# Products of gate and up formed at once, transposed two to three units later, and no accumulating DMA in the first pair block

## Chip, cores and metric

The kernel runs on one core of a Trainium2 chip. The time is device microseconds of one execution, and the measure is the median of several runs. Before the change it is 1096.01 us (three runs, 1095.95 to 1096.87).

## What is computed

The reference is one layer of a streaming encoder on 256 tokens of width 2048: a block of differential attention and convolution, and behind it a gated feed-forward network. The change touches the feed-forward network alone:

```python
hn = rms_norm(h, norm2_g[l])
a = jnp.einsum('bsd,df->bsf', hn, w_gate[l])        # 2048 -> 5632
bu = jnp.einsum('bsd,df->bsf', hn, w_up[l])         # 2048 -> 5632
h = h + jnp.einsum('bsf,fd->bsd', jax.nn.silu(a) * bu, w_down[l])
```

All inputs are float32.

## The kernel before, in words

Every float32 operand is split in two, a rounded high part and a low part that is the difference, and a product of two such operands is three matmuls: high by high, low by high, high by low. The weights are split on the way: the SP queue loads a tile `raw`, ScalarE (ACT) rounds it to `whi` (L305), and VectorE (DVE) subtracts to get `wlo` (L314). For a few tiles, those in `BY_DMA` (L74), `wlo` is made otherwise: ACT writes the rounded negative of `raw` (L308), and a DMA issued from the POOL queue adds `raw` to it in place (L309); the subtraction on DVE then falls away.

The 5632 hidden columns are 11 blocks j of 512, in three groups of 4, 4 and 3 (`FGROUPS`). The blocks of a group are computed one after the other, then the group's share of the down projection is added (`block(w_down, ...)`, in chunks of two rows of 128, four column blocks of 512). Block 0 is computed plainly, gate and then up. Blocks 1 to 10 ("pairs" here, since gate and up are done together) use a fast scheme in `fast_block`: half of the 16 row tiles of the weights go through seven products of sums of tiles instead of eight (units of kind s, four in a pair, 21 matmuls each), the other half plainly (units g for gate and u for up, four each, 12 matmuls each). So a pair has twelve units, and the order is a string: `ORDER` "sggsggsuusuu" for pairs 2 to 10, `FIRST` "gugusgsgsusu" for pair 1. Below, a unit is named by kind and place in its pair, s0, g1, g2, s3 and so on. An s unit costs DVE three subtractions that form the sums of weights (L875 to L877) and two that form low parts (L883, L884), and ACT two roundings (L878, L879); L884 waits for L879, and L879 for L877.

A pair gathers in eight PSUM banks: Q1, Q6, Q7 and Q5 in the pool `acc` (four banks), Q2, Q4, Q3 and QX in the pool `aux` (four banks). A bank is handed out in the order in which banks were given back. When the pair's last s unit is done, `products_done` combines the banks (L962 to L972), and after its last unit `block_done` adds Q3 and QX (two DVE instructions, L980) and multiplies by the activated gate (two more, L983). `transposed` then turns the 128x512 product around on PE in two steps t, each four transposes into one bank `ps_a` (L794), a rounding copy `ahi` on ACT (L796) and a subtraction `alo` on DVE (L798). Here the two steps are called T0 and T1. For pairs their bank is from `aux`, for block 0 from `acc`.

The order on every engine is written out by the program. `run_chunks` goes over the units: ahead of the matmuls of unit t it emits the low parts of unit t+2 and the load, sums and rounding of unit t+3 (for plain chunks, t+2). Work such as `block_done` is a generator, taken one `yield` further at each `resume()`: in a g or u unit or a plain chunk in the middle and at the end, in an s unit behind products 2, 4, 6 and 7, and once more at the end of a pair. `lag(n)` lets n such points go by. If a matmul needs an operand whose `alo` has not been emitted yet, `operand` calls `resume()` until it has.

Of the kernel before, what the change touches and what calls it, by code (L numbers as in the profile page):

```python
# [73 lines left out]
BY_DMA = TWOS[-1:]  # L74

ORDER = "sggsggsuusuu"

FIRST = "gugusgsgsusu"

Q1, Q6, Q7, Q5, Q2, Q4, Q3, QX = range(8)  # L80

PRODUCTS = ((Q1, 0, 5), (Q6, 5, 1), (Q7, 6, 2), (Q5, 4, 3), (Q2, 1, 6), (Q4, 3, 0), (Q3, 2, 4))

HI_AHEAD, LO_AHEAD = 3, 2


def rope_constants():
# [10 lines left out]
def tile_block(  # L98
# [34 lines left out]
    rows = pre.tile([NR, P], F32, tag="rows", name="rows", bufs=1)  # L133
# [79 lines left out]
    def lhs_two(pfx, k):  # L213
        return tuple(lhs.tile([P, 2, S], F32R, tag=f"l{x}", name=f"{pfx}{x}{k}") for x in ("hi", "lo"))
# [20 lines left out]
    def lag(n):  # L235
        for _ in range(n):
            yield
# [538 lines left out]
    def up_done(j, ps):  # L776
        fp = ffn["pool"]
        yield
        aa = []
        for m in range(NM):  # L780
            a = fp.tile([P, N], F32, tag=f"sum{2 + m}", name="a")
            dve.scalar_tensor_tensor(a, ps[m], rstd2[m], sil[m], ALU.mult, ALU.mult)
            aa.append(a)
        yield
        yield from transposed(j, aa)

    def transposed(j, aa):
        for t in range(N // P // 2):
            pool_, tag = (aux_ps, "aux") if j else (acc_ps, "acc")
            pt = pool_.tile([P, 2, S], F32, tag=tag, name="ps_a")  # L790
            for i in range(2):
                for m in range(NM):
                    c = (2 * t + i) * P
                    pe.transpose(pt[:, i, m * P : (m + 1) * P], aa[m][:, c : c + P], ident)  # L794
            hi, lo = lhs_two("a", j * (N // P) + 2 * t)
            act.copy(hi, pt)  # L796
            yield
            dve.tensor_tensor(lo, pt, hi.bitcast(F32), ALU.subtract)  # L798
            for i in range(2):
                actT[j * (N // P) + 2 * t + i] = (hi[:, i, :], lo[:, i, :])  # L800
            yield

# [124 lines left out]
    def fast_block(j, order, after_down):  # L929

        units, sums = [], {}
        left = dict(s=list(range(NS)), g=list(TWOS), u=list(TWOS))
        for kind in order:
            what = left[kind].pop(0)
            c = dict(kind=kind, sums=sums, done=None, first={}, last={})
            if kind == "s":
                c.update(k=what, col=j * N, load=load_pair, round=round_pair, split=split_pair,
                         multiply=multiply_pair, uses=[q for q, _, _ in PRODUCTS], products=PRODUCTS)
            else:
                c.update(ks=what, w=w_gate if kind == "g" else w_up, nk=2, width=N, cols=[(j * N, N)],  # L940
                         rows=slice(what[0], what[1] + 1, what[1] - what[0]), by_dma=what in BY_DMA,
                         load=load_chunk, round=round_chunk, split=split_chunk, multiply=multiply_two,
                         uses=(Q3, QX) if kind == "u" else (Q2, Q4))
            units.append(c)
        assert not any(left.values())
        if after_down:

            units[0]["products"] = PRODUCTS[4:] + PRODUCTS[:4]
        for q in range(8):
            users = [c for c in units if q in c["uses"]]  # L950
            users[0]["first"][q] = users[-1]["last"][q] = True
        [c for c in units if c["kind"] == "s"][-1]["done"] = products_done
        units[-1].update(done=lambda sums: block_done(j, sums), prompt=True)
        chunks.extend(units)
# [20 lines left out]
    def block_done(j, q):  # L975
        while "g" not in halfway:
            yield
        g, u = halfway.pop("g"), halfway.pop("u")
        for m, i in enumerate((Q3, QX)):
            dve.tensor_tensor(u[m], q[i], u[m], ALU.add)  # L980
        yield
        for m in range(NM):
            dve.tensor_tensor(u[m], u[m], g[m], ALU.mult)  # L983
        yield from lag(2)
        yield from transposed(j, u)

    def down_done(g, n, ps):
# [35 lines left out]
    for g, nb in enumerate(FGROUPS):  # L1023
        for j in range(j0, j0 + nb):
            if j:
                fast_block(j, FIRST if j == 1 else ORDER, j == j0)
                continue

            block(w_gate, j * N, range(KD), fh, silu_done)
            block(w_up, j * N, range(KD), fh, lambda ps, j=j: up_done(j, ps))  # L1030
        for n in range(D // N):
            at = len(chunks)
            block(w_down, n * N, range(j0 * 4, (j0 + nb) * 4), fa, lambda ps, g=g, n=n: down_done(g, n, ps))
            for i, c in enumerate(chunks[at:]):
                c["prompt"] = True
                c["spare_raw"] = i % 3 == 2
        j0 += nb
# [32 lines left out]
```

## Time and profile before

| | |
|---|---|
| median of three runs | 1096.01 us |
| the profiled execution, its own time | 1098.23 us |
| its span, first to last instruction | 1096.4 us |
| mean granted TensorE clock | 0.993 of full |
| PE busy | 1063.8 us |
| VectorE (DVE) busy | 844.6 us |
| ScalarE (ACT) busy | 590.3 us |
| HBM read | 200.04 MB |

The feed-forward part runs from about 353 us to the end: block 0 up to 399 us, pairs 1 to 3 up to 540 us, a down stage, pairs 4 to 7 from 630 to 803 us, a down stage, pairs 8 to 10 from 891 to 1022 us, the last down stage. A row of the timeline gives start, duration, engine, line, operation, output and input, shape, and in brackets the idle time of the engine ahead of it with what ended it. Durations of matmuls overlap: in a full stream they start 0.23 us apart. DVE instructions overlap a little as well, so the distance of two starts is the better measure there.

### The profile page before, as it was taken

Reading aid. Unit: us, or ns where it says so; the run is one execution under the profiler, and the core shown is the slowest. Engines: PE = TensorE matmul, PEld = TensorE weight load, DVE = VectorE, ACT = ScalarE, POOL = GpSimd, SP = SyncE. Lnnn points to the kernel's source line nnn. Section 1 sums busy time; section 2 is a strip of 40 time slices with the busy share of each in tenths; the row PEclk is TensorE's granted clock in tenths of the full one; section 3 lists DMA queues with packets and bytes.
Section 4 is the critical chain, followed back from the end, with each engine's and each line's share of the span. In section 5 each row is a group of like instructions: output and inputs, shape, how many; then the busy total and the mean of one; then the engine's idle time right before and its main releaser. Section 6 shows DMA issues by size and latency. Waiting matters only on the chain.

```text
span 1096.4 us, 13237 instructions
## 1 busy us (share of the span) xinstructions
PE 1063.8 (97%) x4834; PEld 873.6 (80%) x4834; DVE 844.6 (77%) x1023; ACT 590.3 (54%) x767; POOL 64.7 (6%) x103
## 2 busy tenths in 40 slices
PE   8999999999999998899999999999999999999998
PEld 7888888877888886687788887877878888778786
DVE  4799989898755779988654699988855589988553
ACT  6544567756764655555443456556533355565332
POOL 0030021201000000000000000000000000000000
PEclk9999999999999999899999999999999999999999
DMA  8756655544345567576455776866646568666561
GB/s 242 251 178 205 192 174 173 154 154 154 135 173 194 171 211 248 181 236 186 147 206 181 247 242 202 248 208 194 186 160 211 201 221 264 213 194 185 170 232 66
DMA packets 121229, 213.50 MB, mean 195 GB/s; under 512 B 7252, under 2 KB 29198, under 8 KB 121164
## 3 DMA queue, kind: packets, MB, share of 16 engines
q1 hardware_dynamic: 117744, 200.56, 54.8%
q0 software_dynamic: 3360, 12.06, 5.9%
q8 instruction: 38, 0.62, 0.2%
q14 instruction: 27, 0.22, 0.1%
q10 hardware_dynamic: 60, 0.03, 0.0%
HBM read 200.04 MB, written 2.10 MB: 184 GB/s over the span
## 4 chain that ended last, share of the span: by engine, by line
PE 85%; DVE 8%; DMA 3%; issue 3%; ACT 1%; POOL 1%; SPq 0%; DVEq 0%; POOLq 0%; ACTq 0%
PE acc L350 16%; PE acc L345 16%; PE acc L344 16%; PE q L917 6%; PE q L918 6%; PE q L923 6%; PE q L900 5%; PE q L902 5%; PE q L901 5%; DVE wlo L314 2%; DVE sum L983 1%; DMA raw<-in_w_in_dram 1%; PE ps_a L794 1%; DVE sum L980 1%; DMA raw<-in_w_gate_dram 1%
## 5 line engine op out<-in xcount | busy, mean ns | idle before, releaser
L305 ACT CAST whi<-raw 128x1024 fp32r<-128x1024 f32 (+1 forms) x297 | 309.9, 1048 | 266.1 <-PE acc L345 171.1
L314 DVE TENSOR_TENSOR wlo<-raw,whi 128x1024 fp32r<-128x1024 f32 (+1 forms) x277 | 335.8, 1218 | 148.5 <-ACT whi L305 148.5
L344 PE MATMUL acc<-whi,ahi 128*128 128x512 f32 x384 | 150.6, 392 | 0.0
L345 PE MATMUL acc<-whi,alo 128*128 128x512 f32 x384 | 150.4, 392 | 0.0
L879 ACT CAST wh<-wt 128x2048 fp32r<-128x2048 f32 x40 | 76.5, 1912 | 104.6 <-DVE wt L877 104.6
L344 PE MATMUL acc<-whi,xhi 128*128 128x512 f32 (+1 forms) x352 | 130.1, 376 | 2.8 <-ACT xhi L219 2.5
L345 PE MATMUL acc<-whi,xlo 128*128 128x512 f32 (+1 forms) x352 | 128.7, 372 | 0.5 <-DVE xlo L220 0.4
L917 PE MATMUL q<-whi,chi 128*128 128x512 f32 x320 | 126.6, 396 | 0.0
L918 PE MATMUL q<-whi,clo 128*128 128x512 f32 x320 | 126.2, 394 | 0.0
L902 PE MATMUL q<-wl,fhi 128*128 128x512 f32 x280 | 110.1, 393 | 2.0 <-DVE wl L884 2.0
L900 PE MATMUL q<-wh,fhi 128*128 128x512 f32 x280 | 110.7, 396 | 0.0
L901 PE MATMUL q<-wh,flo 128*128 128x512 f32 x280 | 109.3, 390 | 0.0
L481 DVE SCALAR_TENSOR_TENSOR y<-upad,cw,y 128x256 f32<-128x256 f32 x240 | 103.3, 480 | 2.8 <-ACT y L474 2.3
L350 PE MATMUL acc<-wlo,ahi 128*128 128x512 f32 x384 | 103.6, 391 | 0.0
L884 DVE TENSOR_TENSOR wl<-wt,wh 128x2048 fp32r<-128x2048 f32 x40 | 91.6, 2290 | 8.4 <-ACT wh L879 8.1
L923 PE MATMUL q<-wlo,chi 128*128 128x512 f32 x320 | 87.3, 395 | 2.4 <-DMA wlo<-raw 2.4
L350 PE MATMUL acc<-wlo,xhi 128*128 128x512 f32 (+1 forms) x352 | 88.5, 377 | 1.2 <-DVE wlo L314 1.2
L345 PEld LDWEIGHTS acc<-whi,alo 128*128 128x128 f32 x384 | 72.7, 189 | 15.2
L344 PEld LDWEIGHTS acc<-whi,ahi 128*128 128x128 f32 x384 | 72.5, 189 | 15.2
L350 PEld LDWEIGHTS acc<-wlo,ahi 128*128 128x128 f32 x384 | 71.6, 188 | 14.5
L344 PEld LDWEIGHTS acc<-whi,xhi 128*128 128x128 f32 x352 | 66.6, 189 | 14.4 <-ACT xhi L219 2.9
L345 PEld LDWEIGHTS acc<-whi,xlo 128*128 128x128 f32 x352 | 66.7, 190 | 11.9 <-DVE xlo L220 0.9
(194 smaller groups left out, 1425.7 us busy)
## 6 DMA issues: line engine op xcount, KB each, us to landing
raw<-in_w_down_dram SPq DMA_DIRECT2D x88, 512.0 KB, 3.7
raw<-in_w_in_dram SPq DMA_DIRECT2D x48, 512.0 KB, 3.6
raw<-in_w_gate_dram SPq DMA_DIRECT2D x48, 512.0 KB, 4.5
raw<-in_w_up_dram SPq DMA_DIRECT2D x48, 512.0 KB, 3.7
wb<-in_w_up_dram SPq DMA_DIRECT2D x40, 512.0 KB, 4.3
wb<-in_w_gate_dram SPq DMA_DIRECT2D x40, 512.0 KB, 5.5
raw<-in_w_out_dram SPq DMA_DIRECT2D x32, 512.0 KB, 3.5
raw<-in_w_in_dram SPq DMA_DIRECT2D x62, 256.0 KB, 3.6
```

The costliest lines, as they stand in the source:

```text
L305: act.copy(c["hi"], c["raw"])
L314: dve.tensor_tensor(c["lo"], c["raw"], c["hi"].bitcast(F32), ALU.subtract)
L344: pe.matmul(ps[m], xhi[:, ms], hi[:, j, :], start=c["first"] and j == 0, stop=False)
L345: pe.matmul(ps[m], xlo[:, ms], hi[:, j, :], start=False, stop=False)
L350: pe.matmul(ps[m], xhi[:, ms], lo[:, j, :], start=False, stop=c["last"] and j == nk - 1)
L481: dve.scalar_tensor_tensor(y[:, ct, :], src, wk, y[:, ct, :], ALU.mult, ALU.add)
L900: pe.matmul(ps, fhi[:, f, p, :], c["hi"][:, w], start=bool(first), stop=False)
L901: pe.matmul(ps, flo[:, f, p, :], c["hi"][:, w], start=False, stop=False)
L902: pe.matmul(ps, fhi[:, f, p, :], c["lo"][:, w], start=False, stop=bool(last))
L917: pe.matmul(ps, x1[:, ms], hi[:, i, :], start=i == 0 and bool(c["first"].get(q)), stop=False)
L918: pe.matmul(ps, x2[:, ms], hi[:, i, :], start=False, stop=False)
L923: pe.matmul(sum_bank(c, q), forms["plain"][k][0][:, ms], lo[:, i, :], start=False, stop=i == 1 and bool(c["last"].get(q)))
```

## The change

In `block_done` the two multiplications follow the two sums without a `yield` between, and five points instead of three (one `yield` and `lag(2)`) pass until T0. In `transposed` two points pass between the copy and `alo`, where one did, and two between the steps (for block 0, one). In pair 1 nothing is split by DMA any more. `FIRST` swaps the units 7 and 9.

```diff
-FIRST = "gugusgsgsusu"
+FIRST = "gugusgsusgsu"
...
+TO_TRANSPOSE = 5
...
             act.copy(hi, pt)
-            yield
+            yield from lag(2)
             dve.tensor_tensor(lo, pt, hi.bitcast(F32), ALU.subtract)
             for i in range(2):
                 actT[j * (N // P) + 2 * t + i] = (hi[:, i, :], lo[:, i, :])
-            yield
+            yield from lag(2 if j else 1)
...
-                         rows=slice(what[0], what[1] + 1, what[1] - what[0]), by_dma=what in BY_DMA,
+                         rows=slice(what[0], what[1] + 1, what[1] - what[0]), by_dma=j > 1 and what in BY_DMA,
...
         for m, i in enumerate((Q3, QX)):
             dve.tensor_tensor(u[m], q[i], u[m], ALU.add)
-        yield
         for m in range(NM):
             dve.tensor_tensor(u[m], u[m], g[m], ALU.mult)
-        yield from lag(2)
+        yield from lag(TO_TRANSPOSE)
         yield from transposed(j, u)
```

## The prediction

> **What bounds the kernel now.** The page shows PE busy nearly all the span, so I asked first what PE waits for.
>
> ```profile
> PE ps_a L794 <- DVE sum L983: 17.3, 19, 4.0
> PE acc L344 <- ACT xhi L219: 2.5, 2, 1.8
> PE q L923 <- DMA wlo<-raw: 2.4, 1, 2.4
> PE q L902 <- DVE wl L884: 2.0, 2, 1.2
> ```
>
> The columns are the total in us, how often, and the longest. Two thirds of PE's waiting is T0 waiting for the multiplications of L983, twice at nearly each of the ten ends of a pair. Next I looked at the stretch of one pair, from one end to the next, where the columns are length, then busy time of PE, PE's weight loads, DVE, ACT and POOL:
>
> ```profile
> 671.20:715.20 44.00, 42.61 (x189) 34.53 (x188) 40.18 (x39) 25.96 (x24) 1.77 (x2) 1.00 0.70 218
> ```
>
> DVE is busy for 40.2 of 44.0 us. It is the second limit, close behind PE, and any idle time that the change puts into DVE's queue counts. So I read the end of pair 4 instruction by instruction, first DVE (the last two rows are the end of pair 5):
>
> ```profile
> 670.73 1.29 DVE L980 TENSOR_TENSOR sum<-q,sum 128x512 f32<-128x512 f32 x2 [0.72 <-PE q L923]
> 671.93 1.22 DVE L314 TENSOR_TENSOR wlo<-raw,whi 128x1024 fp32r<-128x1024 f32 x1
> 673.07 1.22 DVE L875 TENSOR_TENSOR wt<-wb 128x1024 f32<-128x1024 f32 x1
> 674.32 0.69 DVE L876 TENSOR_TENSOR wt<-wb,wt 128x512 f32<-128x512 f32 x1
> 675.05 0.69 DVE L877 TENSOR_TENSOR wt<-wt,wb 128x512 f32<-128x512 f32 x1
> 675.66 1.28 DVE L983 TENSOR_TENSOR sum<-sum,sum 128x512 f32<-128x512 f32 x2
> 678.20 0.69 DVE L798 TENSOR_TENSOR alo<-ps_a,ahi 128x512 fp32r<-128x512 f32 x1 [1.26 <-ACT ahi L796]
> 678.81 1.75 DVE L883 TENSOR_TENSOR wl<-wb,wh 128x1536 fp32r<-128x1536 f32 x1
> 680.48 2.29 DVE L884 TENSOR_TENSOR wl<-wt,wh 128x2048 fp32r<-128x2048 f32 x1
> ...
> 704.68 1.76 DVE L883 TENSOR_TENSOR wl<-wb,wh 128x1536 fp32r<-128x1536 f32 x1 [0.46 <-ACT wh L878]
> ...
> 714.75 1.29 DVE L980 TENSOR_TENSOR sum<-q,sum 128x512 f32<-128x512 f32 x2 [1.04 <-PE q L923]
> ```
>
> then PE and ACT:
>
> ```profile
> 674.89 0.39 PE L902 MATMUL q<-wl,fhi 128*128 128x512 f32 x1
> 676.40 0.33 PE L794 MATMUL ps_a<-ident,sum 128*128 128x128 f32 x1 [1.12 <-DVE sum L983]
> 677.00 0.55 PE L794 MATMUL ps_a<-ident,sum 128*128 128x128 f32 x3 [0.27 <-DVE sum L983]
> 677.30 0.48 PE L900 MATMUL q<-wh,fhi 128*128 128x512 f32 x1
> ...
> 684.07 0.39 PE L900 MATMUL q<-wh,fhi 128*128 128x512 f32 x1
> ```
>
> ```profile
> 675.77 1.90 ACT L879 CAST wh<-wt 128x2048 fp32r<-128x2048 f32 x1 [3.72 <-DVE wt L877]
> 677.58 0.59 ACT L796 CAST ahi<-ps_a 128x512 fp32r<-128x512 f32 x1
> ```
>
> The multiplications stand behind one split (L314, 1.14 us from start to start) and the sums for a later s unit (L875 to L877, 2.59 us), while PE meets T0 after six products of its first unit. A matmul starts 0.23 us after the one before, so without the wait four transposes (0.35 us) and the next product would have begun at 675.12 and 675.47; it began at 677.30. The wait costs 1.83 us, more than the 1.39 named in brackets.
>
> **Part 1: the multiplications at once, T0 later.** Emitted behind the sums, L983 is done 2.4 us after the sums start. T0 is at the sixth point, the middle of g1, over 6 us after the pair's end: that wait is gone at all ten ends. The same 12 instructions are issued, none is added. What is late next? T0's copy `ahi` now stands behind ACT's rounding for the fourth unit ahead, harmless since its `alo` comes only in g2, the eighth point. T1 is at the tenth, in s3 behind its second product, and its `alo` at the twelfth. Two new waits follow from the queues.
>
> First, T1's bank. By the order of banks, s0 takes three of the four `aux` banks, T0 the fourth, and T1 has to take that one again once T0's `alo` is done. DVE gets there after sums 1.20, multiplications 1.21, split 1.14, sums of weights 2.59, L883 1.67, a wait of about 0.35 for L879, L884 2.2, split 1.14 and `alo` 0.69: 12.2 us after the sums' start, in this pair at 682.9. PE reaches T1 at 684.07 less 1.83, less 0.35 (one of the two sets of transposes now comes later), plus six matmuls: 683.3. So at the first end of a group PE doesn't wait, with 0.3 us to spare, and 1.8 us are won.
>
> Second, T1's `alo` now stands on DVE directly behind L877 of s6, and it needs `ahi`, which on ACT stands behind s6's L879, which waits for that very L877. By the ACT rows that is 1.8 us for L879 and 0.6 for `ahi`: DVE idles 2.5 us, with the low parts for s6 queued behind it. DVE's chain from sums to sums was 714.75 − 670.73 = 44.02. Without the waits of 1.26 and 1.04, with 2.5 instead, it is 44.2; the wait of 0.46 goes too if DVE comes there later than ACT, as it then does: 43.8 us. PE alone would take 44.02 − 1.83 = 42.2. So behind the first end of a group DVE sets the pace: at the second its sums start 43.8 − 42.2 = 1.6 us after PE is ready, T1 waits 1.3, and 0.5 us are won; at the third PE loses nearly all again, and 0.2 are won. For this chain the bounds are 43.3 (less idling by 0.5, as the row of 0.46 shows that ACT's own order moves by as much) and 44.8 (a whole whi rounding, about 1 us by half of L879's row, ahead of `ahi`).
>
> At the three ends ahead of a down stage DVE has little else to do (no sums of weights for a next pair), and T0 is in the middle of the third chunk. The row of such an end, and the clock that PE was granted behind it:
>
> ```profile
> PE ps_a L794 <- DVE sum L983: 1.7, 2, 1.4
> 1030.00:1032.00 2.00, 2.00 (x7) 1.62 (x6) 1.62 (x3) 1.23 (x2) 0.00 (x0) 0.60 0.59 216
> 1032.00:1034.00 2.00, 2.00 (x7) 1.41 (x7) 0.48 (x1) 0.00 (x0) 0.00 (x0) 0.54 0.62 199
> ```
>
> With the same 0.4 us on top of the named wait, each of the three gives 2.1 us. At the last one the clock (0.60 and 0.54) was lost for two stretches of 2 us: (0.40 + 0.46) × 2 = 1.7 us more to win there.
>
> But in the last group the down stage has six chunks to a column block, and the sixth reads the rows that T1 makes. T1 is in the middle of chunk 5, its `alo` at the twelfth point, which only the sixth chunk's own demand brings about, behind that chunk's rounding and split of a later tile. From the transposes' end: `ahi` 0.6, the rounding about 0.95 (half of L879's 1.90), split 1.14, `alo` 0.7, so 3.4 with a wake-up of some 0.05. PE has four matmuls and one more, 1.15, before it needs it: PE waits about 2.3 to 2.5 us, once. I take 2.4. Bounds: 0.7 (`alo` alone late) and 3.5.
>
> **Part 2: pair 1 without DMA, its order, block 0's lags.** Rows of DVE, ACT and PE:
>
> ```profile
> 405.81 0.69 DVE L877 TENSOR_TENSOR wt<-wt,wb 128x512 f32<-128x512 f32 x1
> 408.95 0.69 DVE L798 TENSOR_TENSOR alo<-ps_a,ahi 128x512 fp32r<-128x512 f32 x1 [2.45 <-ACT ahi L796]
> ...
> 449.11 1.28 DVE L980 TENSOR_TENSOR sum<-q,sum 128x512 f32<-128x512 f32 x2
> ```
>
> ```profile
> 408.35 0.57 ACT L796 CAST ahi<-ps_a 128x512 fp32r<-128x512 f32 x1
> ```
>
> ```profile
> 410.89 0.40 PE L900 MATMUL q<-wh,fhi 128*128 128x512 f32 x1
> ...
> 454.76 1.50 PE L794 MATMUL ps_a<-ident,sum 128*128 128x128 f32 x4 [3.96 <-DVE sum L983]
> ...
> 464.72 0.39 PE L900 MATMUL q<-wh,fhi 128*128 128x512 f32 x1
> ```
>
> The sums at 449.11 carry no wait, and PE waits 3.96 us for what comes behind them: here DVE is late, and its chain alone decides. The change does four things to it. It moves block 0's first `alo` behind L883 and L884 of s4: the idle 2.45 us shrink to the 0.4 that L884 still waits for ACT (free at 408.35), 2.05 us less. It adds two splits, 2 × 1.14 = 2.3 us, in place of the DMAs. The second `alo`, now between L877 and L883 of s6, saves L884's 0.4 us wait there. And the multiplications move ahead of a split and the sums of weights, which changes no total. So the sums start near 448.9, as before. T0's `alo` ends 12.2 later at 461.1, T1 may begin, and with 0.35 for it and 15 matmuls (3.43) s3 of pair 2 ends at 464.9; before, it began at 464.72 and took 21 × 0.23, so 469.5. That is 4.6 us won. PE's wait of 2.4 us for the DMA and 2.0 for `wl` go as well, but they lie inside the same stretch and win nothing more.
>
> The price is a wait of another kind: Q5 of s4 (its fourth product) gets the bank of block 0's T1, whose `alo` now comes behind the split for g5 and the sums for s6: 408.4 + 2.2 + 0.7 + 1.14 + 2.59 + 0.7 = 415.7, and PE is there at 410.89 + 9 × 0.23 = 413.0, so it waits 2.7 us. DVE's lateness later in the pair covers it; without that cover it would cost its 2.7 less the 1.2 to 2.0 that PE waited for `wl`. The units 7 and 9 cost the same either way round, so the swap I take at nothing: its cover is that weights are loaded units ahead. Two fewer ACT passes and two fewer issues on POOL free engines that nothing waits for here, and on SP the loads behind those two buffers start sooner. At the end of pair 2 DVE is again 1.8 to 2.0 us late by its chain, and T1's wait takes back all of the 1.8: nothing won there.
>
> **The sum.** 4.6 (pair 1 to 2), 0 (2 to 3), 1.8 (4 to 5), 0.5, 0.2, 1.8 (8 to 9), 0.5, three times 2.1 ahead of down stages, 1.7 of clock, less 2.4: 15.0 us. From this I take 1.0 for clock that the new waits lose: a loss costs 1.7, the wait of 2.4 might meet one every second time, and of the nine shorter waits at ends of pairs one did. So 14 us: the profiled execution goes from 1098.2 (span 1096.4) to about 1084, and the runs without profile, which are 2.2 us shorter, from 1096.0 to 1082.
>
> On the clock, the Trainium skill ("TensorE: Matmul & The Clock Gate", The HAM clock gate) says that PE falls to half rate after about one window of 3.4 us of idleness, so gaps under some 3 us are harmless. By that rule the allowance of 1.0 would be nothing and the time 1081. The trace disagrees: the waits of 1.7 us in all were followed by the clocks of 0.60 and 0.54.
>
> **Rivals.**
>
> A, PE sets the pace after all: T1's `alo` idles DVE less than 2.5 us, and all four chained ends win 1.8. Against it are the rows of ACT's 1.90 behind L877; for it, that DVE's busy 40.2 is under PE's 42.2. Then 4 × 1.83 less the 1.2 counted, 6 us more: 1076. Chance 0.15.
>
> B, the chain is at its long bound of 44.8 and the new waits cost clock: four ends lose 1 us more each, the 0.3 us to spare at the first ends go, and the two long waits each lose 1.7: some 8 us less, 1090. For it: several waits of 1.3 to 2.7 us stand where one kind stood. Chance 0.17.
>
> C, slower: DVE's chain becomes longer than the pair was. The place is T1's `alo` in s3, the price is the chain less 44.0 at each of four ends (2 to 3, 5 to 6, 6 to 7, 9 to 10), against 4.6 + 3.6 + 6.3 + 1.7 − 2.4 = 13.8 of firm gains; it decides from a chain of 44.0 + 13.8/4 = 47.5 us, that is an idle DVE of 6.2 us in place of 2.5. At 48.5 the time is 1100. Against it: only one ACT instruction of 1.9 us stands ahead of `ahi` there. Chance 0.04.
>
> D, it does nothing: each wait comes back at another place, T1's bank taking T0's role at the first ends too, so that only pair 1's gain is left and the down stage's wait and lost clock eat it. For it: the 0.3 us to spare are small. The time is 1094 to 1097. Chance 0.06.
>
> **The numbers.** The forecast holds 0.58; its own terms, with the chain from 43.3 to 44.8 and the wait in the down stage from 0.7 to 3.5, reach from 1078 to 1086. With A and B the range is 1075 to 1091. Under 0.2% (2.2 us, about what a measurement of this kernel tells from no change) lies most of D: faster 0.90, the same 0.06, slower 0.04.
>
> **What would show it.** In the new profile PE should wait for L983 nowhere. In its place stand T1's transposes waiting for `alo` (none at the ends of pairs 4 and 8, 1 to 2 us at the others inside a group), Q5 of s4 in pair 1 waiting near 413 for `alo`, and once, in the last group's down stage, a matmul with `alo` waiting over 2 us. DVE should idle 2.5 us ahead of T1's `alo` for `ahi`. The wait of `q` for `wlo` by DMA should be gone, and pairs 5 and 6 about 43.5 us apart. I am wrong if DVE isn't idle there, if T1 waits more than 3 us, or if the down stage's end is won back by a slow clock.

## The result, and the profile after

The changed kernel takes 1083.82 us (median of four runs, 1082.97 to 1084.29) against 1096.44 us before (four runs): a ratio of 0.9884, 95% interval 0.9866 to 0.9901, that is 12.6 us less. The profiled execution fell from 1098.23 to 1082.97 us, its span from 1096.4 to 1081.2.

What PE waits for most, after (total in us, times, longest; the change moved the lines by one or two, so L794 is now L796, L798 is L800, L884 is L886, L980 and L983 are L982 and L984):

```profile
PE ps_a L796 <- DVE alo L800: 4.9, 4, 1.2
PE acc L346 <- ACT xhi L221: 2.8, 2, 2.2
PE acc L347 <- DVE alo L800: 2.3, 1, 2.3
PE q L902 <- DVE alo L800: 2.2, 1, 2.2
PE q L904 <- DVE wl L886: 1.4, 1, 1.4
```

The 17.3 us of T0 behind the multiplications are gone, and so is the wait for the DMA. In their place stand three kinds of wait for an `alo`: T1 for T0's bank, four times 1.2 us; the chunk of the last down stage, 2.3 us; Q5 in pair 1, 2.2 us. The 1.4 us for L886 are in s3 of pair 2, just ahead of T1's first wait. The row of L346 waiting for `xhi` lies ahead of the feed-forward part.

Of the 15.2 us between the spans 1.2 lie ahead of s4 of pair 1 (it starts at 410.89 and 409.71; in a second profile of the changed kernel at 410.51, so most of this isn't the change's); 14.0 lie behind. The same stages in both profiles, each measured from the first matmul of one part to the first of the next; the column "after, again" is that second profile, taken among the experiments. One of the four runs of the changed kernel taken there lasted 1511.0 us at a granted clock of 0.655 and is left out of its figures.

| stage | before | after | after, again | won, as predicted |
|---|---|---|---|---|
| s4 of pair 1 to s0 of pair 3 | 84.76 | 82.34 | 79.50 | 4.6 |
| pair 3 | 43.99 | 42.21 | 43.78 | 0 |
| first down stage | 90.10 | 88.05 | 88.05 | 2.1 |
| pair 5 | 44.01 | 42.20 | 42.22 | 1.8 |
| pair 6 | 44.02 | 43.67 | 43.67 | 0.5 |
| pair 7 | 44.03 | 43.76 | 43.82 | 0.2 |
| second down stage | 90.10 | 88.02 | 88.05 | 2.1 |
| pair 9 | 44.00 | 42.18 | 42.20 | 1.8 |
| pair 10 | 44.03 | 43.69 | 43.69 | 0.5 |
| last down stage, to the end | 73.98 | 72.88 | 72.93 | 1.4 |

The stages of the table won 14.0 us in the first profile and 15.1 in the second; the last column adds up to 15.0.

Pairs 5 and 9 are the first pairs in their groups that turn around a predecessor's product. They win all of their wait, and the next ones hardly anything. The rows of DVE at the ends of pairs 4, 5 and 6, and ahead of the last T1's `alo` in pair 6:

```profile
663.30 1.29 DVE L982 TENSOR_TENSOR sum<-q,sum 128x512 f32<-128x512 f32 x2 [0.71 <-PE q L925]
...
707.08 1.27 DVE L982 TENSOR_TENSOR sum<-q,sum 128x512 f32<-128x512 f32 x2
708.28 1.28 DVE L984 TENSOR_TENSOR sum<-sum,sum 128x512 f32<-128x512 f32 x2
709.48 1.21 DVE L316 TENSOR_TENSOR wlo<-raw,whi 128x1024 fp32r<-128x1024 f32 x1
...
724.33 0.69 DVE L800 TENSOR_TENSOR alo<-ps_a,ahi 128x512 fp32r<-128x512 f32 x1 [2.46 <-ACT ahi L798]
...
750.86 1.27 DVE L982 TENSOR_TENSOR sum<-q,sum 128x512 f32<-128x512 f32 x2
```

From sums to sums DVE takes 43.78 us twice, and only the first sums wait for PE: from there DVE sets the pace. The 2.46 us ahead of T1's `alo` are part of it. PE and ACT in s3 of pair 6:

```profile
717.69 0.42 PE L904 MATMUL q<-wl,fhi 128*128 128x512 f32 x1
719.35 0.66 PE L796 MATMUL ps_a<-ident,sum 128*128 128x128 f32 x4 [1.24 <-DVE alo L800]
```

```profile
721.91 1.91 ACT L881 CAST wh<-wt 128x2048 fp32r<-128x2048 f32 x1 [1.99 <-DVE wt L879]
723.72 0.57 ACT L798 CAST ahi<-ps_a 128x512 fp32r<-128x512 f32 x1
```

T1 waits 1.24 us for its bank, and its copy starts on ACT only when L881 is through, though the transposes were done at about 720.

### The profile page after: what moved, and what is told of

It is laid out like the page before. It is cut to its first block, busy times and chain, and to the rows that moved or that the text cites. A ratio compares the mean times of both kernels' runs of the same rounds, so it can differ in the third digit from the quotient of the medians.

```text
span 1081.2 us, 13236 instructions
## 1 busy us (share of the span) xinstructions
PE 1058.5 (98%) x4834; PEld 871.7 (81%) x4834; DVE 844.8 (78%) x1025; ACT 587.0 (54%) x765; POOL 62.9 (6%) x101
## 4 chain that ended last, share of the span: by engine, by line
PE 79%; DVE 10%; issue 4%; ACT 3%; DMA 2%; POOL 1%; SPq 0%; DVEq 0%; ACTq 0%
PE acc L347 16%; PE acc L346 16%; PE acc L352 16%; PE q L919 5%; PE q L920 5%; PE q L902 5%; PE q L904 5%; PE q L903 5%; PE q L925 5%; DVE wlo L316 3%; ACT wh L881 2%; DVE wt L877 1%; DVE y L483 1%; DMA h<-in_x_dram 1%; PE ps_a L796 1%
## 5 line engine op out<-in xcount | busy, mean ns | idle before, releaser
L346 PE MATMUL acc<-whi,ahi 128*128 128x512 f32 x384 | 149.6, 390 | 0.0
L881 ACT CAST wh<-wt 128x2048 fp32r<-128x2048 f32 x40 | 76.6, 1914 | 127.3 <-DVE wt L879 127.3
L346 PE MATMUL acc<-whi,xhi 128*128 128x512 f32 (+1 forms) x352 | 129.8, 375 | 3.9 <-ACT xhi L221 2.8
L886 DVE TENSOR_TENSOR wl<-wt,wh 128x2048 fp32r<-128x2048 f32 x40 | 91.6, 2290 | 9.2 <-ACT wh L881 9.2
L346 PEld LDWEIGHTS acc<-whi,ahi 128*128 128x128 f32 x384 | 72.1, 188 | 15.2 <-ACT ahi L798 0.2
L346 PEld LDWEIGHTS acc<-whi,xhi 128*128 128x128 f32 x352 | 66.3, 188 | 15.8 <-ACT xhi L221 3.2
```

Of the source, the lines that this page charges most:

```text
L346: pe.matmul(ps[m], xhi[:, ms], hi[:, j, :], start=c["first"] and j == 0, stop=False)
```

## The experiments

Each edit is shown against the kernel named. The times of before are those of the runs on the same chip, and the ratios are to them.

**The multiplications at once, and nothing else.** Against the kernel before:

```diff
         for m, i in enumerate((Q3, QX)):
             dve.tensor_tensor(u[m], q[i], u[m], ALU.add)
-        yield
         for m in range(NM):
             dve.tensor_tensor(u[m], u[m], g[m], ALU.mult)
-        yield from lag(2)
+        yield from lag(3)
```

> The kernel before with one edit: the two multiplications stand directly behind the two sums, and T0 stays at its old point (behind the sixth product of s0); pair 1 keeps its DMA. Queue theory (what PE waits for is decided by where an instruction stands on DVE and ACT): T0's wait of 1.83 us goes at all ends, but T1 in the middle of g1 then waits for T0's bank, since alo of T0 stands behind the sums of weights of s3 and an idle 2 to 2.5 us for its copy: it ends 9.3 us after the sums begin, PE is there after 7.0, so T1 waits about 2 us and the ends between pairs win nothing; the three ends ahead of a down stage win 2.1 each and pair 1's about 3. Together 1087 us. Rival (the place of the multiplications is the whole cure, the later transposes matter little): as the changed kernel, 1084.

Measured: 1094.09 us against 1097.19, ratio 0.9974 (0.9964 to 0.9984), only 3 us. At the end of pair 4 T0 no longer waits, and T1 does; PE, then DVE:

```profile
673.53 0.60 PE L794 MATMUL ps_a<-ident,sum 128*128 128x128 f32 x4
...
678.55 0.66 PE L794 MATMUL ps_a<-ident,sum 128*128 128x128 f32 x4 [1.90 <-DVE alo L798]
```

```profile
677.80 0.69 DVE L798 TENSOR_TENSOR alo<-ps_a,ahi 128x512 fp32r<-128x512 f32 x1 [2.45 <-ACT ahi L796]
```

Seven such waits sum to 14.9 us, 2.1 on the mean, as the queue theory had it, and the rival falls. But the theory's time was 7 us too low. At each end ahead of a down stage T0, still in the middle of the second chunk, waited for the multiplications twice, 0.5 us together, and the first two down stages won 1.1 instead of 2.1. The pairs that follow another in their group took 0.25 us more than before (pair 5 44.26 for 44.01), where the theory had them equal. And pair 1 won under 1 us instead of 3: T1's wait was 3.8 us there, and the clock fell to 0.50 behind it.

**The transposes later, the multiplications as before.** Against the changed kernel:

```diff
             dve.tensor_tensor(u[m], q[i], u[m], ALU.add)
+        yield
         for m in range(NM):
             dve.tensor_tensor(u[m], u[m], g[m], ALU.mult)
-        yield from lag(TO_TRANSPOSE)
+        yield from lag(TO_TRANSPOSE - 1)
```

> The changed kernel with one edit undone: the multiplications come one point after the sums, as before, and T0 stays at the sixth point. Queue theory: the multiplications are done 6.1 us after the sums begin, T0 needs them 6.6 us after the pair's end, so nothing waits for them and the time is the changed kernel's, 1083.8 within 1 us. Rival (the multiplications must stand directly behind the sums): T0 waits 1 to 1.5 us at each of ten ends, 1090 or more.

All other edits of the change stay in. Measured: 1081.50 us, ratio 0.9857 (0.9843 to 0.9872) to before. It is no slower than the change, so the rival falls; it looks 2 us faster, though the intervals of the two ratios overlap. But the theory missed as well: T0 does wait for the multiplications, which now stand in L985.

```profile
PE ps_a L796 <- DVE sum L985: 3.6, 8, 1.8
```

That is 2.1 us at the end of pair 1 and 0.2 to 0.5 at the ends of pairs 2, 5, 6 and 9. In return T1 waits nowhere. The DVE rows behind the end of pair 5 show a reason:

```profile
709.62 0.69 DVE L879 TENSOR_TENSOR wt<-wt,wb 128x512 f32<-128x512 f32 x1
710.23 1.28 DVE L985 TENSOR_TENSOR sum<-sum,sum 128x512 f32<-128x512 f32 x2
711.43 1.75 DVE L885 TENSOR_TENSOR wl<-wb,wh 128x1536 fp32r<-128x1536 f32 x1
713.10 2.28 DVE L886 TENSOR_TENSOR wl<-wt,wh 128x2048 fp32r<-128x2048 f32 x1
```

The multiplications now run while ACT does L881, and L886 has no wait ahead of it, where the changed kernel shows 0.32 us of idling. DVE's chain over pair 6 is 43.36 us (sums at 705.32 and 748.68) instead of 43.78, still with 2.46 us of idling ahead of T1's `alo`; pair 6 takes 42.85 us on PE and 43.67 in the changed kernel. Of what the pairs won 1.6 us were lost again in the last down stage (74.49 us for 72.93), where the clock fell behind the same wait of 2.3 us.

**T1's `alo` later.** Against the changed kernel:

```diff
             act.copy(hi, pt)
-            yield from lag(2)
+            yield from lag(4 if j and t else 2)
```

> The changed kernel with one edit: alo of T1 comes four points behind its copy instead of two, that is in the middle of g4, behind the split for s6. Queue theory: DVE no longer idles 2.45 us ahead of it; its chain from sums to sums falls from about 43.8 to under 42.2, what PE needs, so at the ends of pairs 5, 6 and 9 T1's wait of 1.2 us goes, and the three win 1.5 us each; 4 to 5 us faster, 1079. Rival (DVE's idling lies beside other slack and T1's wait has another cause, the bank or PE's own order): 1083.8, and T1 still waits about 1.2 us in those pairs.

Measured: 1076.96 us, ratio 0.9816 (0.9796 to 0.9836). Pair 6, in the columns length, then busy time of PE, weight loads, DVE, ACT and POOL, in the changed kernel and then here:

```profile
705.75:749.42 43.67, 42.43 (x190) 34.50 (x188) 39.89 (x39) 25.52 (x23) 1.77 (x2) 1.00 0.70 217
```

```profile
702.91:745.09 42.18, 42.18 (x189) 34.58 (x188) 40.09 (x39) 25.60 (x24) 1.77 (x2) 1.00 0.77 237
```

PE has no gap left, with the same work on DVE. The `alo` follows L886 without idling:

```profile
719.44 2.29 DVE L886 TENSOR_TENSOR wl<-wt,wh 128x2048 fp32r<-128x2048 f32 x1 [0.32 <-ACT wh L881]
721.65 0.68 DVE L800 TENSOR_TENSOR alo<-ps_a,ahi 128x512 fp32r<-128x512 f32 x1
```

From 500 to 980 us PE waits for nothing. That DVE's idling ahead of T1's `alo` cost the inner pairs is shown. The gain is near 7 us where 4 to 5 were expected: the ends of pairs 5, 6 and 9 won 1.5 to 1.6 us each as said, and the end of pair 2, which the expectation left out, 1.6 more (pair 3 took 42.22 us, against 43.78 in the second profile of the changed kernel, where T1 waits there too).

**The DMA back in pair 1.** Against the changed kernel:

```diff
-                         rows=slice(...), by_dma=j > 1 and what in BY_DMA,
+                         rows=slice(...), by_dma=what in BY_DMA,
```

> The changed kernel with the accumulating DMA back in pair 1 (units g9 and u11). Queue theory: DVE has two splits less, 2.3 us, in the pair in which it is late; the sums at the end of pair 1 start 2.3 us earlier, the waits of 1.4 (L886) and 1.2 us (T1) in s3 of pair 2 go, and with them the half clock there: 2 to 4 us faster, 1081. Rival (the DMA lands some 8 us after its issue and holds back the unit that reads its low parts): PE waits 2 us or more for a tile wlo in pair 1 and the time is 1084 to 1086.

Measured: 1081.72 us, ratio 0.9860 (0.9846 to 0.9875), and PE's waits from 420 to 470 us:

```profile
PE ps_a L796 <- DVE alo L800: 1.2, 1, 1.2
PE q L925 <- DMA wlo<-raw: 0.3, 1, 0.3
```

The sums start 35.1 us after s4 of pair 1 does, against 37.3 in the changed kernel (446.16 − 411.07 and 447.00 − 409.71), which is the two splits. The wait for L886 is gone; T1's 1.2 us stay, against expectation, since PE comes earlier too (this reason is argued). The intervals of this ratio and of the changed kernel's overlap, but the profile places the gain: from s4 of pair 1 to pair 3 it takes 77.44 us, against 79.50 in the second profile of the changed kernel, the clock at full speed in both. The DMA is hardly late: it costs 0.3 us, at u11, where it cost 2.4 at g7 before. Here the swap of units matters, for it makes g9 the DMA's tile in place of g7. In the two profiles with the DMA at g7 PE waited 2.4 us (before) and 1.6 us (the multiplications alone) for it, in the four with the DMA at g9 at most 0.4 us in all of pair 1. No run has the old order with the rest of the change and the DMA, so what removed that wait isn't shown.

**Block 0's lags as before.** Against the changed kernel:

```diff
             act.copy(hi, pt)
-            yield from lag(2)
+            yield from lag(2 if j else 1)
```

> The changed kernel with the old lags in block 0's two transposes (one point between copy and alo, one between the steps). Queue theory: Q5's wait of 2.2 us in s4 of pair 1 goes, but DVE idles 2.4 us again for the copy, and since DVE is what is late at the end of pair 1, its sums start 2 us later and the time is 1 to 2 us longer, 1085 to 1086. Rival (PE's wait in s4 is lost time): 2.2 us shorter, 1081.6.

Measured: 1086.76 us, ratio 0.9910 (0.9895 to 0.9924). PE's wait for Q5 is gone, and DVE's idling is back:

```profile
407.94 0.69 DVE L800 TENSOR_TENSOR alo<-ps_a,ahi 128x512 fp32r<-128x512 f32 x1 [2.45 <-ACT ahi L798]
```

The sums start 39.8 us after s4 (450.11 − 410.31), 2.5 later than in the changed kernel. In this pair an idle DVE is lost time and an idle PE isn't. Of the 3 us by which the time is longer, more than expected, the profile puts only a part here: the stage from s4 of pair 1 to pair 3 takes 83.75 us, 1.4 more than in the first profile of the changed kernel, in which the clock fell there too. Another 1.7 us lie in the last down stage (74.56 us for 72.88), which the edit doesn't touch and where the clock fell in this profile (0.78, 0.50 and 0.86 from 1028 to 1034 us).

**The old order of pair 1.** Against the changed kernel:

```diff
-FIRST = "gugusgsusgsu"
+FIRST = "gugusgsgsusu"
```

> The changed kernel with the old order of pair 1 (g7 and u9 instead of u7 and g9), still without DMA there. Queue theory: the same instructions in the same number on every queue, so 1083.8 within 1 us and the same waits. Rival (the order of the loads from the two weight matrices matters): a wait for a tile raw or whi appears in pair 1, 1085 or more.

Measured: 1083.81 us, ratio 0.9875 (0.9859 to 0.9891), with the same waits. Without the DMA in pair 1 the swap does nothing that can be seen.

**The last pair's transposes one point earlier.** Against the changed kernel:

```diff
-        yield from lag(TO_TRANSPOSE)
+        yield from lag(TO_TRANSPOSE - (j == FF // N - 1))
```

> The changed kernel with the transposes of the last pair (block 10) one point earlier, the fifth instead of the sixth. Queue theory: T1's alo then comes at the eleventh point, the end of the fifth chunk, ahead of the sixth chunk's rounding and split; PE's wait of 2.3 us for alo in the last down stage goes, T0 waits under 0.5 us: 2 us faster, 1081.8. Rival (the wait is the latency of transposes, copy and subtraction itself): no change, 1083.8.

Measured: 1081.44 us, ratio 0.9857 (0.9840 to 0.9874). The last down stage's wait:

```profile
PE acc L347 <- DVE alo L800: 0.5, 1, 0.5
```

It was the place in DVE's queue, not the latency of the work. The last down stage takes 71.08 us instead of 72.93, nearly the whole gain.

**The changed kernel again.**

> The changed kernel itself on this chip, for comparison: 1083.8 us within 1.5, and the same waits, with Q5 in pair 1 about 2.2, T1 1.2 at the ends of pairs 5, 6 and 9, and 2.3 in the last down stage. Whether PE falls to half clock behind s3 of pair 2 again is open; if it does not, T1 should wait at the end of pair 2 as well.

Measured: 1083.18 us (median of three), ratio 0.9878 (0.9858 to 0.9897). Its profile has no half clock behind s3 of pair 2, and T1 does wait at the end of pair 2: PE's waits for T0's bank are five, 6.2 us in all.

**Three edits together.** The edits of T1's `alo`, of the DMA and of the last pair, in one kernel.

> The changed kernel with three edits at once: alo of T1 in the middle of g4, the accumulating DMA back in pair 1, the last pair's transposes one point earlier. Queue theory: each takes away a wait of another place, so what they won singly adds up: 7 us from the first, about 2 from each of the others, 1072 to 1074 us, and PE waits at no end of a pair over 0.6 us; left are Q5's 2 us in pair 1 and T1's after pair 1. Rival (they share one slack, DVE's): little better than the first edit alone, 1076 to 1077.

Measured: 1075.40 us, ratio 0.9805 (0.9790 to 0.9819): less was won than the sum. The last down stage's wait was back at 1.9 us: with four points between copy and `alo`, T1's `alo` comes after the sixth chunk's demand even if the transposes are earlier. So the first edit undid the third; and the clock fell behind that wait (0.72 and 0.50 from 1016 to 1020 us), which made the stage 74.08 us long.

**The same with the multiplications one point later.**

> The three edits, and the multiplications one point behind the sums again, as before the change. Queue theory: with DVE's chain below what PE needs, the 0.35 us per pair that the later place saved DVE no longer count, and T0 waits some 0.2 to 0.3 us at seven ends for the multiplications: 1 to 2 us longer than with the three edits. Rival (the later place is better in itself): 1 to 2 us shorter.

Measured: 1075.75 us, ratio 0.9808 (0.9794 to 0.9823): no difference to be told. T0 waits twice at the end of pair 1 and twice at the last pair's, 1.7 us in all, and not at the seven ends expected; T1's wait is gone.

**The three edits kept apart.** Against the three edits:

```diff
-            yield from lag(4 if j and t else 2)
+            yield from lag(4 if t and 0 < j < FF // N - 1 else 2)
```

> The three edits, but alo of T1 keeps its two points in the last pair, so that the first edit no longer undoes the third: there it came at the thirteenth point, after the sixth chunk of the down stage had asked for it. Queue theory: the wait of 1.9 us in the last down stage falls to about 0.5 as in the run with the early transposes alone, and where that wait lost clock the loss goes too: 1.4 to 3 us shorter than the three edits, 1072.5 to 1074. Rival (the wait is made by something else once the pairs are faster): 1075.4.

Measured: 1072.51 us against 1097.14, ratio 0.9782 (0.9768 to 0.9795). The wait is 0.5 us, and the last down stage takes 71.20 us instead of 74.08, which is the whole gain. This is the fastest version, some 11 us under the changed kernel.

## Why the prediction was right

The forecast was 1082.0, the time is 1083.8, and most steps hold one by one. One step between them doesn't: the forecast took the profiled execution to be 2.2 us longer than the others, from the one pair of numbers before. After the change it is the shortest of its four, 1082.97 us, where 1084 was forecast.

T0's wait was said to cost 1.83 us and to go at all ends. Pairs 5 and 9 became 1.8 us shorter, and no wait for L984 is left.

T1's bank and its `alo` were said to idle DVE 2.5 us and to make its chain 43.8 us; measured are 2.46 and 43.78. T1 waits 1.2 us where 1.3 was said, and pairs 6, 7 and 10 won 0.35, 0.27 and 0.34 where 0.5, 0.2 and 0.5 were. The run with the later `alo` shows the cause: take the idling away and the pairs take PE's 42.18 us (42.2 was said to be PE's own need).

The down stages won 2.05 and 2.08 for 2.1. The last one won 1.1 where 1.4 was said. Its wait was 2.31 for 2.4; PE's row of it, in the changed kernel:

```profile
1025.58 0.50 PE L347 MATMUL acc<-whi,alo 128*128 128x512 f32 x1 [2.31 <-DVE alo L800]
```

The allowance for lost clock let this wait meet a loss every second time. Of the seven profiles that have it at 2.3 us, two show a slower clock behind it, and there the stage is 1.6 to 1.7 us longer, as the price of 1.7 had it.

Q5's wait was said to be 2.7 us and covered. It was 2.2, and the run with block 0's old lags shows the cover: without the wait the time is longer. The swap at nothing is right for the change as it stands, without the DMA.

Pair 1 and the clock are where the first profile differs from the steps, though not from the sum. T0's `alo` ended 49.5 us after s4 of pair 1 began, where 50.2 was reckoned. PE's waiting for it, though, came in two parts: T1's wait, which the prediction has (1.2 us measured), and ahead of it one for L886, which it doesn't name (1.4 us). Then the clock fell, the columns being as in the windows above with the clock third from the end:

```profile
458.00:460.00 2.00, 0.76 (x5) 0.73 (x5) 2.00 (x3) 1.84 (x2) 1.08 (x1) 0.57 0.71 243
460.00:462.00 2.00, 2.00 (x7) 1.61 (x6) 1.73 (x3) 0.17 (x1) 0.00 (x0) 0.50 1.01 281
462.00:464.00 2.00, 2.00 (x6) 1.54 (x5) 0.00 (x0) 2.00 (x2) 0.00 (x0) 0.50 1.01 201
464.00:466.00 2.00, 2.00 (x8) 1.60 (x7) 1.75 (x2) 1.16 (x2) 0.00 (x0) 0.73 0.07 12
```

By the clock that is (0.50 + 0.50 + 0.27) × 2 = 2.5 us and, of the 0.76 us in which PE was busy in the first row, 0.43 × 0.76 = 0.3, so 2.8 us; the allowance of 1.0 for all such losses, and the price of 1.7 for one, were too small for this place. The kernel before shows as much: behind PE's wait of 3.96 us at the same end its clock was 0.50 from 454 to 460 us and 0.90 up to 462, which is 2.8 us by the same reckoning. The prediction didn't list that loss; its 4.6 us, counted from the old start of s3, contain it. In the changed kernel more than half of the loss was given back: with PE late, DVE caught up, T1 didn't wait at the end of pair 2, and pair 3 took 1.8 us less than said. In the second profile the clock held, and both stages stand near what was forecast: 5.3 us won for 4.6, and 0.2 for 0. So the total agreed twice, once with two errors that mostly cancel, and that was luck.

One thing the prediction didn't see. It let the removed wait rest on both edits, the multiplications at once and the later transposes. The runs part them: the first alone moves the wait to T1 and wins 3 us; the rest of the change without it wins all, and the profile of that run has pair 6 shorter by 0.8 us. It reckoned the DMA's removal rightly as 2.3 us more for DVE in a pair where DVE is late, and the wait for the DMA as worth nothing there; so by its own terms this part of the change was a loss, which it doesn't say. The run with the DMA back is 2 us faster than the change: with the units swapped, that part of the change costs time.

Open is when the clock falls. In the two profiles of the changed kernel the wait for Q5 (2.2 and 2.0 us) was followed by a slower clock once and not the other time, and so were the 1.4 and 1.2 us behind pair 1. Nothing was tried that sets it. Open, too, is which of the later points does the work: the place of T0, the two points ahead of `alo` and the two between the steps were not tried apart.

## What to carry to other kernels

When PE waits for a step on a second engine that is itself over 90% busy, moving the consumer later frees PE only as far as that engine's chain allows: add up its chain from one round to the next with every idle that the new order makes, and compare it with PE's need. Look for an instruction that stands in an in-order queue directly behind the producer of a long step on a third engine and needs something queued behind that step: here one such idle of 2.46 us per pair ate most of the gain behind the first end of a group, and two points of delay gave it back. Test the edits of a bundle apart: of these the later transposes are what is left as doing the work, with the others taken back one by one; block 0's lags helped; the swap did nothing without the DMA; the multiplications at once won 3 us alone and none beside the later transposes; and the DMA's removal cost time.

## What the hardware showed that was not expected

Short waits can be followed by a much longer loss of clock: behind 1.4 and 1.2 us, with one matmul between, the clock was about half for some 7 us in one profile (0.57, 0.50, 0.50 and 0.73 from 458 to 466 us) and full in another profile of the same program, which had the same two waits. That the waits set it off isn't shown. A loss of clock need not all show in the time: where DVE sets the pace, as in pairs 2 and 3 here, of 2.8 us lost 1.6 came back at the next wait.
